# The router's index work put behind all four rankings, with expert units between its steps

## The chip, the cores and the metric

The kernel runs on one core of one Trainium2 chip. The metric is device microseconds of one execution; the median of three runs before the change is 3709.58 us (3703.13 to 3713.91).

The core's engines have their own in-order instruction queues and meet only through semaphores: TensorE (PE; its weight loads are PEld), VectorE (DVE), ScalarE (ACT), GpSimd (POOL) and SyncE (SP, which here only issues DMAs). ACT and POOL issue some DMAs too. An instruction that waits for something holds up everything behind it on its engine.

## The reference, cut to what matters

Two transformer blocks on 512 tokens of width 1024. The change lies in the first block's expert layer (`peer`), between a gated mixer before it and a second block of attention after it:

```
q = (hb @ w_q).reshape(T, 8, 2, 128)                    # 8 heads, two halves
s = einsum('thpc,hpnc->thpn', q, sub_keys)              # 128 scores per half
sub_s, sub_i = top_k(s, 16)
cand = (sub_s[:, :, 0, :, None] + sub_s[:, :, 1, None, :]).reshape(T, 8, 256)
top_s, top_i = top_k(cand, 16)                          # 16 of the 256 sums
k1 = take_along_axis(sub_i[:, :, 0], top_i // 16); k2 = take_along_axis(sub_i[:, :, 1], top_i % 16)
g = softmax(top_s)                                      # the gates
act = gelu(einsum('td,thkd->thk', hb, expert_u[k1 * 128 + k2])) * g
out = einsum('thk,thkd->td', act, expert_v[k1 * 128 + k2])
```

## The kernel before, in words

The expert layer (`experts`, L576) treats the 512 tokens in four tiles of 128. Tiles 0 to 2 (384 tokens) go the dense way: products of these tokens with all 16384 rows of `expert_u`, later weighted by a gate matrix and multiplied with `expert_v`. Tile 3 goes the sparse way: its 128 tokens' chosen rows are gathered from HBM by 256 indirect DMAs of 512 KB (`gathered`, L693), each followed by one VectorE instruction.

**Units.** The dense first half is 128 equal units (`up_products`, L732). One unit loads 512 KB of `expert_u` in two DMAs (`wr<-eu`, issued on SP), splits it into a rounded part `wh` (ACT cast, L120) and a rest `wl` (L122, on POOL; on VectorE while `dve_lo` holds the tag, as in the gate-matrix stage), runs 24 matmuls of 128x384 into a PSUM tile `u` (two of them), and evicts `u` through a Gelu on ACT into `hb` (L745), stored by an ACT DMA. Units have no data in common with the routing: they are filler, issued by `tick(n)` (L592), which adds n to a counter and traces one unit for each whole number. After the context stage the rest is traced in one loop (L619).

**Stages that call `tick`.** In `route` (L750): the scores (2 and 14 x R1 = 0.5), the ranking (R2 = 0.7 before each of 32 heads' rankings), 1.0, and the gate matrix (48 x R3 = 0.6, in the loop at L884). In `context` (L1446, the second block's context tokens), R4 = 0.53 before each of its 104 weight products (`mm`). Then 6 more in `unit` calls and the rest.

**The ranking, tile by tile (L814), in the order 3, 0, 1, 2.** Per tile VectorE builds 64 candidate sums per head (`cand`, L818), and ranks each head (`top16`, L667: MAX8, FIND_INDEX8, MATCH_REPLACE8, MAX8, FIND_INDEX8). Then comes the tile's index work (L826 to L847): small mask arithmetic, then twice a compare (L842) and a product (L844) of 128x2048 elements and a reduction (L846) into `kt`. Tile 3's two results make `xid`, the row numbers of the gathers. After the fourth tile the softmax runs over all tiles at once: a subtraction (L856, VectorE), an Exp on ACT (L857), a sum, a reciprocal and a product (VectorE), the copy of tile 3's gates on ACT (L862). Then nine transposes on PE (L867: two `kt` and one `e` per dense tile), each evicted on ACT into `k0T`, `k1T` or `k2T` (L868), and `kw`. The gate-matrix stage takes over their SBUF pool when it is closed.

**What sets the order.** Each engine's queue is laid out ahead of time by a planner: a list scheduler that takes the instructions in traced order as priority, simulates their durations with a cost model, and lets a later one go first where it is ready sooner in that simulation. `self.here(ins)` (L689) takes an instruction out of this: it is queued behind everything traced before it on its engine (later work may still be placed ahead of it). In the kernel before, the gathers and the VectorE instructions that follow them are so pinned; the Exp, the transposes and their evictions are not. `gathered` is a generator: its first gather is traced at the first `self.sparse` call (L900).

Of the kernel before, what the change touches and what calls it, by code (L numbers as in the profile page):

```python
# [8 lines left out]
F32 = mybir.dt.float32  # L9
# [4 lines left out]
U32 = mybir.dt.uint32  # L14
AF = mybir.ActivationFunctionType
# [1 line left out]
AX = mybir.AxisListType  # L17
PSUM = bass.MemoryType.PSUM

R1, R2, R3, R4, R5, R6 = 0.5, 0.7, 0.6, 0.53, 0.9, 0.12  # L20
PC = 2
MB, MD, MR = 4, 2, 1.15
TG, NT = 4, 8
# [11 lines left out]
GS = 32768.0  # L35
# [32 lines left out]
class Kern:  # L68
# [681 lines left out]
    def route(self, ws, pu, tick):  # L750
        nc, a, h = self.nc, self.a, self.h
        with ExitStack() as s1:
            ip = self.pool("ip", scope=s1)
            pr = self.pool("pr", 1, PSUM, s1)
# [7 lines left out]
            kT = [ip.tile([128, TD, 2], F16 if i < 2 else F32, name="k%dT" % i) for i in range(3)]  # L762
# [3 lines left out]
            with ExitStack() as s2:  # L766
                rp = self.pool("r1", scope=s2)
# [32 lines left out]
            def ax(t, pat, shape):  # L800
                return t.rearrange(pat, o=1).to_broadcast(shape)

            S4 = [128, 8, 16, 16]
            with ExitStack() as s2:
                rp = self.pool("r2", scope=s2)
# [5 lines left out]
                srcs = {}  # L811
                tva = rp.tile([128, 4, 8, 16], F32, name="tva")
                gates = self.sp_.tile([128, 128], F32, name="gates")
                for n in (3, 0, 1, 2):  # L814
                    cand = rp.tile([128, 8, 64], F32, name="cand", tag="cand", bufs=2)
                    for p0, i0, ni, nj in ROWS:
                        S = [128, 8, ni, nj]
                        nc.vector.tensor_tensor(cand[:, :, p0:p0 + ni * nj].rearrange("p h (i j) -> p h i j", j=nj),  # L818
                                                ax(vals[:, n, :, 0, i0:i0 + ni], "p h (i o) -> p h i o", S),
                                                ax(vals[:, n, :, 1, 0:nj], "p h (o j) -> p h o j", S), op=OP.add)  # L820
                    tv = tva[:, n]
                    ti = rp.tile([128, 8, 16], U32, name="ti", tag="ti", bufs=2)
                    for hd in range(8):
                        tick(R2)
                        self.top16(rp, cand[:, hd], 64, tv[:, hd, :], ti[:, hd, :], "mr2")
                    pos = rp.tile([128, 8, 16], F32, name="pos", tag="pos", bufs=2)  # L826
                    nc.vector.tensor_copy(pos, ti)
                    msk = rp.tile([128, 8, 16], F32, name="msk", tag="msk", bufs=2)
# [10 lines left out]
                    src = []  # L839
                    for w_, (at, table, cmp) in enumerate(((pos, st16, OP.is_ge), (col, io16, OP.is_equal))):  # L840
                        oh = rp.tile(S4, F32, name="oh", tag="oh", bufs=2)
                        nc.vector.tensor_tensor(oh, ax(at, "p h (r o) -> p h r o", S4),  # L842
                                                table.rearrange("p (o r) i -> p o r i", o=1).to_broadcast(S4), op=cmp)
                        nc.vector.tensor_tensor(oh, oh, ax(idf[:, n, :, w_, :], "p h (o i) -> p h o i", S4), op=OP.mult)  # L844
                        kt = rp.tile([128, 8, 16], F32, name="kt", tag="kt", bufs=8)
                        nc.vector.tensor_reduce(out=kt, in_=oh, axis=AX.X, op=OP.add)  # L846
                        src.append(kt)  # L847
                    if n == 3:
                        xid = self.sp_.tile([128, 128], I32, name="xid")
                        nc.vector.scalar_tensor_tensor(xid, src[1].rearrange("p h r -> p (h r)"), 128.0,  # L850
                                                       src[0].rearrange("p h r -> p (h r)"), op0=OP.mult, op1=OP.add)
                        self.sunits = self.gathered(xid, gates, htok)
                    srcs[n] = src
                e = rp.tile([128, 32, 16], F32, name="e")
                tv = tva.rearrange("p n h r -> p (n h) r")
                nc.vector.tensor_tensor(e, tv, tv[:, :, 0:1].to_broadcast([128, 32, 16]), op=OP.subtract)  # L856
                nc.scalar.activation(out=e, in_=e, func=AF.Exp)  # L857
                sm = rp.tile([128, 32], F32, name="sm")
                nc.vector.tensor_reduce(out=sm, in_=e, axis=AX.X, op=OP.add)
                nc.vector.reciprocal(sm, sm)  # L860
                nc.vector.tensor_tensor(e, e, ax(sm, "p (h o) -> p h o", [128, 32, 16]), op=OP.mult)
                nc.scalar.copy(gates, e[:, 24:32].rearrange("p h r -> p (h r)"))  # L862
                for n in range(3):
                    tps = pr.tile([128, 3, 128], F32, name="tps", tag="tps", bufs=2)
                    for i in range(3):
                        src = srcs[n][i] if i < 2 else e[:, 8 * n:8 * n + 8]
                        nc.tensor.transpose(tps[:, i, :], src.rearrange("p h r -> p (h r)"), self.ident)  # L867
                        nc.scalar.activation(out=kT[i][:, n * 128:(n + 1) * 128, :], in_=ax(tps[:, i, :], "p (t o) -> p t o", [128, 128, 2]),  # L868
                                             func=AF.Copy, scale=GS if i == 2 else 1.0)
                nc.scalar.copy(kw[0], kT[2])  # L870
                nc.vector.tensor_tensor(kw[1], kT[2], kw[0], op=OP.subtract)
            s12.close()
# [1 line left out]
            with ExitStack() as s2:  # L874
                rp = self.pool("r3", 2, scope=s2)
# [8 lines left out]
                for b in range(TD // 32):  # L884
                    stg = rp.tile([128, 128, 32], F32, name="stg", tag="stg")
                    for c in range(32 // NT):
                        t0 = b * 32 + c * NT
                        oh = []
                        for i in range(2):
                            o = rp.tile([128, NT, 128], F16, name="oh%d" % i, tag="oh%d" % i)  # L890
# [1047 lines left out]
```

## Time and profile before

| | us |
|---|---|
| runs shown | 3709.58 median, 3703.13 to 3713.91 |
| profiled execution, its own time | 3703.34 |
| its span, first to last instruction | 3701.6 |
| PE busy | 3415.2 (92% of the span) |
| VectorE busy | 2369.2 (64%) |
| ACT busy | 1564.2 (42%) |
| POOL busy | 1407.8 (38%) |
| mean granted TensorE clock | 0.966 |

The stages around the change, in us from the span's start: scores about 570 to 728, ranking and index work 728 to 857, gate matrix 857 to 1084, context from there to about 1690, the last units and the first products of the second half to 1745. From 1744 on PE runs the dense second half without a break until 2201; the second block follows.

Readings to keep apart: "busy" of PE is modelled, since matmuls are pipelined; a wait is put down to the instruction that released it last; a granted clock of 1.00 is 2.4 GHz, and 0.5 would be 1.2 GHz throughout.

### The profile page before, as it was taken

To read this page: it belongs to the slowest core of one execution; us is meant where nothing else is said; L and a number is where in the kernel's file an instruction comes from. 1 tells how busy PE (TensorE), PEld (TensorE's weight loads), DVE (VectorE), ACT (ScalarE), POOL (GpSimd) and SP (SyncE) were. 2 spreads that over 40 slices of the span, in tenths; PEclk is the share of its full clock that TensorE was granted. 3 is DMA by queue.
4 is the path that set the end of the run, shared out by engine and by line. 5 is a ranking of instruction groups with operands and counts; after the bars stand their busy time and mean duration, and the time that the engine had idled before them with its cause. 6 is when DMAs were issued, how large, how long until landed. Compare 5 with 4: busy or idle time off the path is not lost.

```text
span 3701.6 us, 54609 instructions
## 1 busy us (share of the span) xinstructions
PE 3415.2 (92%) x20219; PEld 3074.3 (83%) x20219; DVE 2369.2 (64%) x4572; ACT 1564.2 (42%) x2940; POOL 1407.8 (38%) x1178
## 2 busy tenths in 40 slices
PE   6999999978889998897999999899999979999998
PEld 5889788877788988897999998778878877787777
DVE  7876865698867765666777775444255664433554
ACT  3323223235654374642333333444346443442663
POOL 2210114352235667565222211554425335542442
PEclk9999999989999998998999999999999989999999
DMA  7667644337877856578999993322211321212122
GB/s 274 217 204 263 219 159 152 107 125 269 298 265 242 301 194 241 184 273 294 355 342 337 327 328 111 103 69 69 77 52 55 134 82 63 75 67 67 54 72 99
DMA packets 273243, 668.18 MB, mean 181 GB/s; under 512 B 25424, under 2 KB 88016, under 8 KB 270160
## 3 DMA queue, kind: packets, MB, share of 16 engines
q1 hardware_dynamic: 220256, 469.43, 36.9%
q0 software_dynamic: 36864, 134.23, 10.1%
q10 hardware_dynamic: 15856, 61.02, 4.3%
q8 instruction: 159, 2.61, 0.3%
q14 instruction: 108, 0.88, 0.1%
HBM read 601.47 MB, written 63.11 MB: 180 GB/s over the span
## 4 chain that ended last, share of the span: by engine, by line
PE 65%; DVE 13%; DMA 7%; issue 7%; ACT 5%; POOL 3%; SPq 0%; POOLq 0%; ACTq 0%; DVEq 0%
PE mm L95 16%; PE acc L95 12%; PE gm L95 10%; PE u L95 8%; PE cm L95 4%; PE uq L95 2%; PE sc L95 2%; PE pv L1168 2%; DMA wr<-eu 2%; PE tp L1138 2%; PE pv L95 2%; PE tp L95 1%; DVE wm L212 1%; DVE wl L122 1%; POOL wl L122 1%
## 5 line engine op out<-in xcount | busy, mean ns | idle before, releaser
L122 POOL TENSOR_TENSOR wl<-wr,wh 128x512 fp32r<-128x512 f32 (+3 forms) x358 | 499.0, 1411 | 452.3 <-ACT wh L120 437.6
L120 ACT CAST wh<-wr 128x512 fp32r<-128x512 f32 (+3 forms) x546 | 355.8, 665 | 576.2 <-PE mm L95 201.5
L95 PE MATMUL u<-hh,wh 128*128 128x384 f32 (+1 forms) x1040 | 361.5, 348 | 31.8 <-ACT hb L745 31.6
L95 PE MATMUL u<-hh,wl 128*128 128x384 f32 (+1 forms) x1040 | 360.2, 347 | 9.7 <-DVE wl L122 8.9
L95 PE MATMUL u<-hl,wh 128*128 128x384 f32 (+1 forms) x1040 | 358.8, 345 | 0.0
L95 PE MATMUL acc<-ah,vh 128*128 128x384 f32 x1024 | 343.9, 336 | 8.8 <-ACT hb L745 8.8
L95 PE MATMUL acc<-al,vh 128*128 128x384 f32 x1024 | 343.3, 335 | 0.9 <-DVE al L122 0.9
L95 PE MATMUL acc<-ah,vl 128*128 128x384 f32 x1024 | 343.2, 335 | 0.0
L714 POOL DMA_INDIRECT sg<-ev,xid x128 | 153.3, 1198 | 311.4 <-DVE sacc L729 258.0
L120 ACT CAST vh<-vr 128x1024 fp32r<-128x1024 f32 x128 | 134.6, 1052 | 316.8 <-issue 145.0
L714 POOL DMA_INDIRECT sg<-ur,xid x128 | 146.8, 1147 | 270.2 <-DVE sg L212 250.7
L95 PE MATMUL mm<-hh,wh 128*128 128x512 f32 (+2 forms) x608 | 239.3, 398 | 9.1 <-DVE sm L432 4.2
L122 DVE TENSOR_TENSOR wl<-wr,wh 128x1024 fp32r<-128x1024 f32 (+4 forms) x188 | 179.5, 972 | 101.2 <-ACT wh L120 100.1
L95 PE MATMUL mm<-hh,wl 128*128 128x512 f32 (+2 forms) x608 | 238.9, 393 | 5.6 <-DVE wl L122 4.5
L95 PE MATMUL mm<-hl,wh 128*128 128x512 f32 (+2 forms) x608 | 238.8, 393 | 5.4 <-POOL hl L122 5.4
L122 DVE TENSOR_TENSOR vl<-vr,vh 128x1024 fp32r<-128x1024 f32 x128 | 158.3, 1237 | 128.4 <-ACT vh L120 126.9
L95 PEld LDWEIGHTS u<-hh,wh 128*128 128x128 f32 x1040 | 203.6, 196 | 34.8 <-ACT hb L745 32.9
L95 PEld LDWEIGHTS u<-hh,wl 128*128 128x128 f32 x1040 | 203.3, 196 | 13.1 <-DVE wl L122 11.3
L729 DVE SCALAR_TENSOR_TENSOR sacc<-sg,wts,sacc 128x1024 f32<-128x1024 f32 x128 | 189.3, 1479 | 22.5 <-DMA sg<-ev,xid 19.0
L95 PEld LDWEIGHTS u<-hl,wh 128*128 128x128 f32 x1040 | 203.4, 196 | 0.4
L95 PEld LDWEIGHTS acc<-ah,vh 128*128 128x128 f32 x1024 | 193.1, 189 | 9.3 <-ACT hb L745 9.1
L95 PEld LDWEIGHTS acc<-al,vh 128*128 128x128 f32 x1024 | 193.1, 189 | 1.1 <-DVE al L122 1.1
(713 smaller groups left out, 9837.2 us busy)
## 6 DMA issues: line engine op xcount, KB each, us to landing
wr<-eu SPq DMA_DIRECT2D x256, 256.0 KB
vr<-ev SPq DMA_DIRECT2D x128, 512.0 KB
wm<-wmod SPq DMA_DIRECT2D x88, 512.0 KB
wr<-w SPq DMA_DIRECT2D x164, 256.0 KB
wr<-wA SPq DMA_DIRECT2D x80, 512.0 KB
wrc<-w SPq DMA_DIRECT2D x79, 512.0 KB
wrg<-w SPq DMA_DIRECT2D x104, 256.0 KB
hd<-hb ACTq DMA_DIRECT2D x64, 384.0 KB
```

The source lines that it names most:

```text
L95: ins = self.nc.tensor.matmul(ps, l, r, start=first and i == 0, stop=last and i == 2)
L120: nc.scalar.copy(hi, x)
L122: eng.tensor_tensor(lo, x, hi.bitcast(F32), op=OP.subtract)
L212: return self.nc.vector.scalar_tensor_tensor(chunk, chunk, 1.0, row, op0=OP.mult, op1=OP.mult, accum_out=dst)
L714: self.here(nc.gpsimd.indirect_dma_start(t, None, tabs[i], bass.IndirectOffsetOnAxis(idx[:, j:j + 1], 0)))
L729: self.here(nc.vector.scalar_tensor_tensor(acc, t, wts[:, j:j + 1], acc, op0=OP.mult, op1=OP.add))
L1138: nc.tensor.transpose(t[:, (b - i) * 128:(b - i + 1) * 128], p[:, b * 128:(b + 1) * 128], self.ident)
L1168: nc.tensor.matmul(o[:, lo:hi], v(b), pt[k][:, b, lo:hi], start=i == 0 and k == 0, stop=i == len(parts) - 1 and k == 1)
```

## The change

The loop over tiles is cut into three inner functions. `best(n)` is the candidate sums and the ranking of a tile; `keys_of(n)` its index work; `turn(n, i)` one transpose with its eviction, both now pinned with `self.here`. The order becomes: `best(3)`, `keys_of(3)` and `xid`; `best(0)`, `best(1)`, `best(2)`; the subtraction; `keys_of(0)`; the Exp (pinned); `keys_of(1)`; sum, reciprocal, product; two transposes of tile 0; `keys_of(2)`; the gates' copy, now on VectorE; the third transpose of tile 0 and the three of tile 1; `tick(R8)`; the three of tile 2. The tile `ti` becomes one slice per token tile (`tia`).

The units are dealt out anew: R2 from 0.7 to 0.45; a `tick(R7 / 2)` of 2 units twice in each `keys_of`; R8 = 2 units before the last transposes; R3 from 0.6 to 0.55; R4 from 0.53 to 0.47.

```diff
--- before.py
+++ after.py
@@ -17,7 +17,7 @@
 AX = mybir.AxisListType
 PSUM = bass.MemoryType.PSUM
 
-R1, R2, R3, R4, R5, R6 = 0.5, 0.7, 0.6, 0.53, 0.9, 0.12
+R1, R2, R3, R4, R5, R6, R7, R8 = 0.5, 0.45, 0.55, 0.47, 0.9, 0.12, 4, 2
 PC = 2
 MB, MD, MR = 4, 2, 1.15
 TG, NT = 4, 8
@@ -811,18 +811,22 @@
                 srcs = {}
                 tva = rp.tile([128, 4, 8, 16], F32, name="tva")
                 gates = self.sp_.tile([128, 128], F32, name="gates")
-                for n in (3, 0, 1, 2):
+                tia = rp.tile([128, 4, 8, 16], U32, name="tia")
+                order = (3, 0, 1, 2)
+
+                def best(n):
                     cand = rp.tile([128, 8, 64], F32, name="cand", tag="cand", bufs=2)
                     for p0, i0, ni, nj in ROWS:
                         S = [128, 8, ni, nj]
                         nc.vector.tensor_tensor(cand[:, :, p0:p0 + ni * nj].rearrange("p h (i j) -> p h i j", j=nj),
                                                 ax(vals[:, n, :, 0, i0:i0 + ni], "p h (i o) -> p h i o", S),
                                                 ax(vals[:, n, :, 1, 0:nj], "p h (o j) -> p h o j", S), op=OP.add)
-                    tv = tva[:, n]
-                    ti = rp.tile([128, 8, 16], U32, name="ti", tag="ti", bufs=2)
                     for hd in range(8):
                         tick(R2)
-                        self.top16(rp, cand[:, hd], 64, tv[:, hd, :], ti[:, hd, :], "mr2")
+                        self.top16(rp, cand[:, hd], 64, tva[:, n, hd, :], tia[:, n, hd, :], "mr2")
+
+                def keys_of(n):
+                    ti = tia[:, n]
                     pos = rp.tile([128, 8, 16], F32, name="pos", tag="pos", bufs=2)
                     nc.vector.tensor_copy(pos, ti)
                     msk = rp.tile([128, 8, 16], F32, name="msk", tag="msk", bufs=2)
@@ -842,31 +846,51 @@
                         nc.vector.tensor_tensor(oh, ax(at, "p h (r o) -> p h r o", S4),
                                                 table.rearrange("p (o r) i -> p o r i", o=1).to_broadcast(S4), op=cmp)
                         nc.vector.tensor_tensor(oh, oh, ax(idf[:, n, :, w_, :], "p h (o i) -> p h o i", S4), op=OP.mult)
+                        tick(R7 / 2)
                         kt = rp.tile([128, 8, 16], F32, name="kt", tag="kt", bufs=8)
                         nc.vector.tensor_reduce(out=kt, in_=oh, axis=AX.X, op=OP.add)
                         src.append(kt)
+                    return src
+
+                e = rp.tile([128, 32, 16], F32, name="e")
+                sm = rp.tile([128, 32], F32, name="sm")
+
+                def turn(n, i):
+                    if i == 0:
+                        tpss[n] = pr.tile([128, 3, 128], F32, name="tps", tag="tps", bufs=2)
+                    src = srcs[n][i] if i < 2 else e[:, 8 * n:8 * n + 8]
+                    self.here(nc.tensor.transpose(tpss[n][:, i, :], src.rearrange("p h r -> p (h r)"), self.ident))
+                    self.here(nc.scalar.activation(out=kT[i][:, n * 128:(n + 1) * 128, :],
+                                                   in_=ax(tpss[n][:, i, :], "p (t o) -> p t o", [128, 128, 2]),
+                                                   func=AF.Copy, scale=GS if i == 2 else 1.0))
+
+                tpss = {}
+                for n in order:
+                    best(n)
                     if n == 3:
+                        src = keys_of(3)
                         xid = self.sp_.tile([128, 128], I32, name="xid")
                         nc.vector.scalar_tensor_tensor(xid, src[1].rearrange("p h r -> p (h r)"), 128.0,
                                                        src[0].rearrange("p h r -> p (h r)"), op0=OP.mult, op1=OP.add)
                         self.sunits = self.gathered(xid, gates, htok)
-                    srcs[n] = src
-                e = rp.tile([128, 32, 16], F32, name="e")
                 tv = tva.rearrange("p n h r -> p (n h) r")
                 nc.vector.tensor_tensor(e, tv, tv[:, :, 0:1].to_broadcast([128, 32, 16]), op=OP.subtract)
-                nc.scalar.activation(out=e, in_=e, func=AF.Exp)
-                sm = rp.tile([128, 32], F32, name="sm")
+                srcs[0] = keys_of(0)
+                self.here(nc.scalar.activation(out=e, in_=e, func=AF.Exp))
+                srcs[1] = keys_of(1)
                 nc.vector.tensor_reduce(out=sm, in_=e, axis=AX.X, op=OP.add)
                 nc.vector.reciprocal(sm, sm)
                 nc.vector.tensor_tensor(e, e, ax(sm, "p (h o) -> p h o", [128, 32, 16]), op=OP.mult)
-                nc.scalar.copy(gates, e[:, 24:32].rearrange("p h r -> p (h r)"))
-                for n in range(3):
-                    tps = pr.tile([128, 3, 128], F32, name="tps", tag="tps", bufs=2)
-                    for i in range(3):
-                        src = srcs[n][i] if i < 2 else e[:, 8 * n:8 * n + 8]
-                        nc.tensor.transpose(tps[:, i, :], src.rearrange("p h r -> p (h r)"), self.ident)
-                        nc.scalar.activation(out=kT[i][:, n * 128:(n + 1) * 128, :], in_=ax(tps[:, i, :], "p (t o) -> p t o", [128, 128, 2]),
-                                             func=AF.Copy, scale=GS if i == 2 else 1.0)
+                for i in range(2):
+                    turn(0, i)
+                srcs[2] = keys_of(2)
+                nc.vector.tensor_copy(gates, e[:, 24:32].rearrange("p h r -> p (h r)"))
+                turn(0, 2)
+                for i in range(3):
+                    turn(1, i)
+                tick(R8)
+                for i in range(3):
+                    turn(2, i)
                 nc.scalar.copy(kw[0], kT[2])
                 nc.vector.tensor_tensor(kw[1], kT[2], kw[0], op=OP.subtract)
             s12.close()
```

## Rows read from the trace of the kernel before

**Rows 1.** The page's forty slices of the span, in tenths: PE.
```profile
PE   6999999978889998897999999899999979999998
```
**Rows 2.** Stretches by time: busy us (instructions) of PE, PEld, DVE, ACT, POOL; clock; DMA.
```profile
780.00:800.00 20.00, 20.00 (x118) 20.00 (x117) 20.00 (x47) 8.43 (x16) 16.27 (x11) 1.00 0.48 170
800.00:820.00 20.00, 6.05 (x35) 5.72 (x34) 20.00 (x64) 0.45 (x1) 0.88 (x1) 0.78 0.14 47
```
**Rows 3.** Waits of PE and ACT, 725 to 860: total us, times, longest.
```profile
PE u L95 <- ACT hb L745: 22.5, 1, 22.5
PE tps L867 <- ACT k0T L868: 5.4, 1, 5.4
...
ACT e L857 <- DVE e L856: 25.6, 1, 25.6
```
**Rows 4.** ACT in order of time: start, duration; idle time before, its releaser.
```profile
731.55 0.48 ACT L745 ACTIVATE hb<-u 128x384 f32<-128x384 f32 x1
...
798.16 0.49 ACT L745 ACTIVATE hb<-u 128x384 f32<-128x384 f32 x1
...
826.04 0.63 ACT L857 ACTIVATE e<-e 128x512 f32<-128x512 f32 x1 [25.59 <-DVE e L856]
...
840.15 0.30 ACT L862 COPY gates<-e 128x128 f32<-128x128 f32 x1 [4.84 <-DVE e L861]
```
**Rows 5.** VectorE in order of time: index work, softmax and the next stage's first.
```profile
764.35 1.37 DVE L850 SCALAR_TENSOR_TENSOR xid<-kt 128x128 int32<-128x128 f32 x1
...
772.71 0.22 DVE L827 CAST pos<-ti 128x128 f32<-128x128 uint32 x1
...
794.41 2.27 DVE L846 TENSOR_REDUCE kt<-oh 128x128 f32<-128x2048 f32 x1
...
803.37 0.22 DVE L827 CAST pos<-ti 128x128 f32<-128x128 uint32 x1
...
816.65 2.27 DVE L846 TENSOR_REDUCE kt<-oh 128x128 f32<-128x2048 f32 x1
...
825.34 0.67 DVE L856 TENSOR_TENSOR e<-tva 128x512 f32<-128x512 f32 x1
...
842.84 2.27 DVE L846 TENSOR_REDUCE kt<-oh 128x128 f32<-128x2048 f32 x1
...
856.55 0.69 DVE L891 TENSOR_TENSOR oh<-iota,k0T 128x1024 f16<-128x1024 f16 x1 [2.35 <-PE tps L867]
```
**Rows 6.** VectorE groups by form, 728 to 766: count, busy us, mean ns.
```profile
L844 DVE TENSOR_TENSOR oh<-oh,idf 128x2048 f32<-128x2048 f32 x2 | 6.6, 3282 | 0.0
...
L838 DVE CAST col<-mi 128x128 f32<-128x128 uint32 x1 | 1.2, 1174 | 0.0
```
**Rows 7.** The same groups, 802 to 826.
```profile
L844 DVE TENSOR_TENSOR oh<-oh,idf 128x2048 f32<-128x2048 f32 x2 | 4.6, 2276 | 0.0
...
L838 DVE CAST col<-mi 128x128 f32<-128x128 uint32 x1 | 0.2, 217 | 0.0
```
**Rows 8.** The tile wl, 728 to 860, its POOL instructions: ns min/median/max.
```profile
L122 POOL TENSOR_TENSOR wl<-wr,wh x38: 1287/1306/3434, 731.8 to 834.9; 128x512 fp32r<-128x512 f32 x38
```
**Rows 9.** The chain by line: 857 to 1084, 1108 to 1663, 1663 to 1745.
```profile
by line: DMA wr<-eu 24.0%; PE u L95 23.4%; DVE ow L895 8.9%; PE gps L904 8.3%; DVE oh L891 7.4%; ACT stg L906 7.0%; DVE wl L122 6.9%; issue 5.1%; DVE sg L212 4.4%; ACT wh L120 1.6%; DVE sacc L729 1.6%; ACT hb L745 1.4%; DVEq L122 0.1%; DVE 
...
by line: PE u L95 26.2%; PE cm L95 25.4%; issue 9.4%; DMA sg<-ev,xid 5.9%; DVE wlc L122 3.8%; DMA wrc<-w 2.9%; POOL wl L122 2.8%; POOL sz L1172 1.5%; ACT whc L120 1.3%; DMA sg<-ur,xid 1.3%; PE ct L1138 1.1%; DMA hd<-hb 1.1%; DVE sacc L729 1
...
by line: DMA vr<-ev 30.5%; POOL wl L122 16.0%; issue 10.0%; DMA wr<-eu 8.7%; PE u L95 7.3%; ACT wh L120 3.0%; POOL sg L714 2.7%; ACT vh L120 2.6%; PE cm L95 2.4%; SPq L87 2.3%; ACT hb L745 1.9%; DVE vl L122 1.5%; PE ct L171 1.5%; ACT sq L15
```
**Rows 10.** The tile hb: units evicted from 857 to 1084, 1108 to 1663, 1663 to 1745.
```profile
L745 ACT ACTIVATE hb<-u x30: 483/491/493, 857.7 to 1081.6; 128x384 f32<-128x384 f32 x30
...
L745 ACT ACTIVATE hb<-u x51: 478/487/496, 1125.6 to 1662.6; 128x384 f32<-128x384 f32 x51
...
L745 ACT ACTIVATE hb<-u x12: 468/485/492, 1662.6 to 1743.8; 128x384 f32<-128x384 f32 x12
```
**Rows 11.** POOL in order of time: the first gather.
```profile
836.40 1.14 POOL L714 DMA_INDIRECT sg<-ur,xid  x1 [0.16 <-DVE mi L836]
```

## The prediction

> **What bounds the kernel now.** I read the page's slices first: PE is at 9 tenths almost everywhere, so what counts is where PE stands still [rows 1]. The ninth and tenth slices, 740 to 833 us, are the lowest run of the first half's middle, and there VectorE is full. The stretches show why they differ: from 780 to 800 PE, PEld and VectorE are all at 20.00 of 20 us; from 800 to 820 PE has 6.05, and its clock has fallen from 1.00 to 0.78 [rows 2]. The waits name it: once, for 22.5 us, the units' matmuls waited for `hb`, the eviction that frees their PSUM tile; ACT, which does it, waited 25.6 us for the subtraction before the softmax [rows 3]. So the Exp stood in ACT's queue ahead of evictions that were due. In order of time: units evicted every 4.16 us ((798.16 - 731.55) / 16 intervals), then nothing until the Exp at 826.04 [rows 4]. VectorE was behind the plan: it subtracts at 825.34 [rows 5].
>
> After it VectorE finishes the last tile's index work at 845.1 (842.84 + 2.27), and the gate matrix starts only at 856.55, since its tiles take over the pool that the transposes still read [rows 5]. In between lie 5.4 us of PE for an eviction of a transpose [rows 3]. Last, the later stages: units' matmuls are 23.4%, 26.2% and 7.3% of the chains of the gate matrix, the context and the tail [rows 9].
>
> **Units, counted.** Traced before the gate matrix: 2 + 7 + 22.4 = 31 before; 2 + 7 + 14.4 + 16 + 2 = 41 after. In the gate matrix (with the `tick(1.0)`) 30 become 27, in the context 55 become 49, at its end 6 stay, and the rest falls from 6 to 5. Ten units move ahead, out of three later stages. The total of PE's work is unchanged: a gain is PE's standing still that goes, less what the later stages get back by losing filler.
>
> **The PE side of the new ranking.** The eviction at 731.55 is the 10th unit's, so 22 units precede the pinned Exp (31 in all), 4 more the first transposes, 4 the next, 2 the last. The 31st's eviction comes at 731.55 + 21 x 4.16 = 819, the 39th's at 852, the 41st's at 860.6. Does the pitch hold? It did, 16 times in a row, beside contended index work with POOL at 16.27 of 20 us and DMA at 170 GB/s [rows 2, 4]; ten more units bring ten more pairs of `wl` on POOL, ten `hb`, twenty casts and twenty SP loads at the same rate, and ACT has 8.43 of 20 us busy. So the units cost PE what they cost later, and SP's queue is only passed earlier by the same loads.
>
> **The VectorE side.** Work is the same but for the copy of the gates. Tile 0's index work took 24.0 us (772.71 to 796.68) with POOL splitting beside it, tile 1's 15.5 us (803.37 to 818.92) with POOL idle [rows 5]; the planner laid some of the next ranking between them, which I estimate at 2.3 and 1.2 us (its last candidate sum and a few small instructions). So 21.7 against 14.3. The products show it, 3282 against 2276 ns [rows 6, 7]. With units beside all four tiles I take 21 us for each. Tile 3's ends with `xid` at 765.7. Three rankings follow: before, the stretch from there to 825.34 held just them and the index work of tiles 0 and 1, so they take 59.6 - 21.7 - 14.3 = 23.6 us, and I add 1 for candidate sums that now meet POOL: 790, the subtraction to 791. Then tile 0 to 812, tile 1 to 833, tile 2 with softmax (about 4 us) to 858. The Exp needs 791 and has 819: its wait is gone. The first transposes (behind the 35th unit, about 836) need 812, tile 1's need 833 and stand at 853. Late next are two things: the product of the softmax, which the planner may put behind most of tile 2's index work (about 855) while the third transpose stands behind the 39th unit at 852, and tile 2's keys at 858 against 860.6.
>
> The Trainium skill, "SBUF — State Buffer", section "Who interferes with whom", says that a VectorE instruction with two SBUF inputs and a GpSimd one that reads SBUF exclude each other for a whole instruction. That speaks against this change, which puts POOL's splits beside index work that ran alone. The 3282 and 2276 ns agree; a rule of whole instructions, taken at its worst, is the end of my first rival.
>
> **The sum** (in the profiled execution's own time, 3703.34; the median shown is 6.2 us above it, and I carry the difference over).
> - Start of the gate matrix. PE ends the 41st unit about 860; 3 us for the third transpose's wait and 2.5 us for nine pinned transposes, each pair in one tile waiting for an ACT eviction: 866 instead of 856.55, +9.5. Bounds: +4 (no wait) and +17 (index work at 24 us a tile). A wait of a pinned transpose holds PE's and ACT's queues behind it, thus units and evictions, unless the planner put some ahead; their nearest row is the 5.4 us [rows 3].
> - Gathers. The first is queued on POOL behind the last split traced before it, now the 41st unit's: about 855 instead of 836.40 [rows 11], and the six at the start (3 MB) land as the gate matrix begins instead of ahead of it. Their consumer on VectorE has the copies behind it. Before, such loads met in the 5.4 us stall; I take nothing extra, bounds 0 and 6.
> - The gates' copy: ACT loses a wait of 4.84 us [rows 4] which by then held no matmul back; VectorE gains 0.2 us, or 1.2 if it meets POOL, by the nearest conversion of that size, 217 and 1174 ns [rows 6, 7]. The gates are first used after sixteen gathers. Nothing in the sum. (By the same section of the Trainium skill such a copy can take the shared port and block; a 1174 ns conversion beside POOL agrees.)
> - Gate matrix: 30 units over 227 us. Their matmuls, loads and splits are 23.4 + 24.0 + 6.9 = 54.3% of the chain [rows 9, 10], 123 us or 4.1 a unit, an upper end, since the loads also wait for the gathers. 2.5 units fewer (the 42nd is half begun), at 3 us: -7. Bounds 0 and -12.
> - Context: 26.2 + 2.8% of 555 us over 51 units is 3.15 us a unit [rows 9, 10]; 6 fewer: -19. Bounds: -6 (only a third comes back, filler having covered waits) and -25 (all 4.16).
> - Tail: one unit fewer: 16.0 + 8.7 + 7.3% of 82 us over 12 units is 2.2 us, and since no other products run beside the rest I take the pitch: -4; bounds -2 and -8.
>
> Together 9.5 - 7 - 19 - 4 = -20.5: 3682.8 for the profiled execution, 3689 as a median. As a check: 22.5 + 5.4 us of waits and a few us at the lower clock go, some 5 come, so PE is 25 to 28 us less idle there, and the later stages lose 4 to 8 of it.
>
> **Rivals.**
> 1. *VectorE is the bound of the new ranking.* If index work beside POOL takes 24 us a tile, as tile 0's whole stretch did, tile 2's keys come at 867 and PE and ACT stand behind the pinned transposes: the gate matrix starts 17 us late, 3697. At the worst each of about a dozen two-input or converting instructions of a tile waits for a whole split of 1.31 us [rows 8]: 14.3 + 12 x 1.31 = 30 us a tile, keys at 885, a start 31 us late and no gain, 3710. For: four tiles, not two and a half, meet POOL. Against: 24.0 us is the longest seen, with other work in it.
> 2. *All ten units come back in full.* 10 x 4.16 = 41.6, less 7.5: 3675. For: `u` and `cm`, PE's two kinds of product, make half of the context's chain [rows 9]. Against: the gate matrix's chain holds loads and copies too.
> 3. *The change doesn't do what it says*: another stall of some 20 us in the ranking takes the old one's place, the planner having set the pinned evictions too early for VectorE. Then +9.5 + 20 - 30 = about 3709. Against: the slack of 17 to 28 us worked out for all but the last two.
> 4. *Slower: the later stages do not give back.* If the context and the gate matrix are paced by loads, dependencies and VectorE, the units there are filler and cost nothing. The later start and gathers stay: 9.5 + 5 = +14, 3724. It decides from under 1.4 us returned per moved unit (14 / 10). For: loads and gathers have 24.0% of one chain and 5.9 + 2.9% of the other. Against: the `u` share of both [rows 9].
>
> **How the numbers follow.** Forecast 0.58, rivals 0.15, 0.12, 0.06 and 0.09. A measurement of this kernel can tell about 0.3%, 11 us: faster means below 3698.5. Forecast gives 0.54 of that (its bounds reach past the line a little), rival 2 all, rival 1 half: 0.74. Same: 0.04 + 0.07 + 0.06 = 0.17. Slower 0.09. The range holds forecast, rivals 1 and 2: 3672 to 3705.
>
> **What would show it.** In the trace after: no wait of PE for `hb` over 5 us between 728 and 866; the Exp directly after its table load; 41 evictions before the gate matrix's first compare, at 862 to 870; index work at 20 to 22 us in all four dense and gathered tiles; the context's stretch 15 to 22 us shorter. It would be wrong if the first compare came after 875, if the context kept its length with more idle PE, or if a pinned transpose took the Exp's place as the long wait.

## The result, and the profile after

The changed kernel takes 3669.81 us (median of 4 runs, 3662.54 to 3677.99) against 3707.3 us (median of 4, 3703.13 to 3713.91): a ratio of 0.991, with a 95% interval of 0.989 to 0.993. Timed again on another occasion beside the kernel before, it took 3668.8 against 3706.09 us, 0.9905 (0.9885 to 0.9926). So it is faster by 37 us, and its median lies 19 us below the forecast of 3689. It is also 2 us below the lower end of the range, 3672 to 3705; taken as a ratio from the 3709.58 that the forecast started from, it is 3676 (3669 to 3684), inside it. The result is at the range's edge either way. The profiled execution took 3676.05 us, 27.3 less than the one before (3703.34).

PE's slices of the changed kernel, in tenths, answer to [rows 1]. The ninth slice shows where to look: it had 7 tenths and has 9. (A slice is 92.5 us, so the prediction's 740 to 833 us is the ninth slice alone, not the ninth and tenth.)

```profile
PE   6999999998788989888999998999999979999998
```

The same two stretches as in [rows 2], 4 us later because the stages ahead took 4 us longer (their code is the same). Columns are the stretch, its length, busy us (instructions) of PE, PEld, DVE, ACT, POOL, granted clock, DMA share, GB/s:

```profile
784.00:804.00 20.00, 20.00 (x118) 20.00 (x117) 20.00 (x83) 7.60 (x15) 15.18 (x10) 1.00 0.48 156
804.00:824.00 20.00, 20.00 (x117) 20.00 (x117) 20.00 (x14) 7.39 (x15) 17.10 (x11) 1.00 0.59 195
```

The second had 6.05 us of PE at a clock of 0.78; now it is full at 1.00. What PE and ACT waited for, the changed kernel's answer to [rows 3] (PE from 728 to 880, where this is its only wait, ACT from 725 to 870; one line of each):

```profile
PE tps L862 <- DVE e L883: 5.1, 1, 5.1
...
ACT k2T L863 <- PE tps L862: 5.5, 2, 4.7
```

The 22.5 us for `hb` and ACT's 25.6 us for the subtraction are gone. What is late instead is the third transpose, which waits for the softmax's product. ACT in order of time [rows 4]:

```profile
735.91 0.48 ACT L745 ACTIVATE hb<-u 128x384 f32<-128x384 f32 x1
...
823.31 0.49 ACT L745 ACTIVATE hb<-u 128x384 f32<-128x384 f32 x1
823.82 1.28 ACT L879 ACT_TABLE_LOAD   x1
825.11 0.63 ACT L879 ACTIVATE e<-e 128x512 f32<-128x512 f32 x1
...
856.96 0.48 ACT L745 ACTIVATE hb<-u 128x384 f32<-128x384 f32 x1
...
873.32 0.49 ACT L745 ACTIVATE hb<-u 128x384 f32<-128x384 f32 x1
```

These are the evictions of the 10th, 31st, 39th and 41st unit. From the 10th to the 31st the pitch is (823.31 - 735.91) / 21 = 4.16 us, from there to the 39th 4.21; the last two take 16.4 us between the transposes. VectorE in order of time [rows 5]:

```profile
793.23 0.67 DVE L877 TENSOR_TENSOR e<-tva 128x512 f32<-128x512 f32 x1
...
857.59 2.29 DVE L851 TENSOR_REDUCE kt<-oh 128x128 f32<-128x2048 f32 x1
...
860.89 0.69 DVE L883 TENSOR_TENSOR e<-e,sm 128x512 f32<-128x512 f32 x1
861.62 0.23 DVE L887 COPY gates<-e 128x128 f32<-128x128 f32 x1
...
876.37 0.69 DVE L915 TENSOR_TENSOR oh<-iota,k0T 128x1024 f16<-128x1024 f16 x1
```

From the subtraction's start to the last reduction's end 66.7 us go to three tiles, 22.2 each. The product stands behind all of the last tile's index work. The first gather [rows 11] is behind the 41st unit's split:

```profile
858.85 1.14 POOL L714 DMA_INDIRECT sg<-ur,xid  x1 [0.17 <-issue]
```

**The ledger.** The chain of waits lists next to nothing of the changed kernel's gate matrix and context, so [rows 9] have no counterpart, and I count by stretches. They are cut where the work is the same in both kernels: first conversion of the ranking, first compare of the gate matrix, its last eviction, first addition of the context's merge, last product of the dense second half (its start, at 2284.8 before; the 2201 given above is not yet the end of that work). The kernel before:

```profile
730.50:856.50 126.00, 97.10 (x538) 95.28 (x537) 119.98 (x354) 39.72 (x78) 74.37 (x46) 0.89 0.45 157
856.50:1082.80 226.30, 191.13 (x1489) 176.12 (x1488) 199.92 (x313) 139.04 (x187) 58.94 (x40) 0.94 0.78 279
1082.80:1671.40 588.60, 530.39 (x3626) 514.59 (x3625) 388.73 (x571) 297.05 (x583) 365.64 (x298) 0.94 0.69 238
1671.40:2284.80 613.40, 592.21 (x3386) 588.84 (x3385) 452.16 (x611) 214.69 (x315) 153.07 (x138) 0.98 0.86 309
```

The changed kernel:

```profile
734.80:876.40 141.60, 136.49 (x777) 135.33 (x776) 133.06 (x356) 55.90 (x109) 110.45 (x65) 0.98 0.58 188
876.40:1088.40 212.00, 174.63 (x1409) 159.85 (x1408) 194.53 (x309) 133.28 (x179) 54.04 (x39) 0.95 0.80 284
1088.40:1650.80 562.40, 506.32 (x3491) 488.82 (x3491) 387.79 (x572) 288.51 (x566) 339.09 (x288) 0.96 0.72 244
1650.80:2254.40 603.60, 586.61 (x3362) 581.91 (x3361) 449.06 (x611) 212.80 (x312) 151.11 (x136) 0.99 0.87 312
```

PE's instruction counts add up to 9039 in both: the four stretches hold the same work. At 24 matmuls a unit, the ranking gained 239 / 24 = 10.0 units, and the others gave up 3.3, 5.6 and 1.0. Length less PE's busy time is PE's idle time: 28.9, 35.2, 58.2, 21.2 us before, 5.1, 37.4, 56.1, 17.0 after. The ranking lost 23.8 us of idling for its ten units, and the three stages that gave them up together idle 110.5 us instead of 114.6. That is the gain: -27.9 us of idle time, and -6.8 us of busy time for the same instructions, at a clock of 0.98 instead of 0.89 in the ranking and 0.96 instead of 0.94 in the context.

### The profile page after: what moved, and what is told of

The parts are those of the page before. It is cut to its first block, busy times and chain, and to the rows that moved or that the text cites. A ratio compares the mean times of both kernels' runs of the same rounds, so it can differ in the third digit from the quotient of the medians.

```text
span 3674.3 us, 54614 instructions
## 1 busy us (share of the span) xinstructions
PE 3414.1 (93%) x20219; PEld 3070.9 (84%) x20219; DVE 2371.5 (65%) x4567; ACT 1564.0 (43%) x2941; POOL 1410.4 (38%) x1184
## 4 chain that ended last, share of the span: by engine, by line
PE 39%; DMA 5%; issue 4%; DVE 4%; ACT 3%; POOL 1%; SPq 0%; POOLq 0%; ACTq 0%; DVEq 0%
PE acc L95 11%; PE gm L95 9%; PE mm L95 8%; PE pv L1192 2%; PE sc L95 2%; PE tp L1162 2%; PE pv L95 2%; PE tp L95 1%; DMA vr<-ev 1%; DMA wr<-w 1%; DMA wro<-w 1%; POOL wl L122 1%; PE sc L1417 0%; PE sc L1422 0%; ACT wh L120 0%
## 5 line engine op out<-in xcount | busy, mean ns | idle before, releaser
L122 POOL TENSOR_TENSOR wl<-wr,wh 128x512 fp32r<-128x512 f32 (+3 forms) x364 | 506.6, 1408 | 417.6 <-ACT wh L120 403.7
L95 PEld LDWEIGHTS acc<-ah,vl 128*128 128x128 f32 x1024 | 193.2, 189 | 1.3 <-DVE vl L122 1.3
```

What stands on the lines that cost most here:

```text
L95: ins = self.nc.tensor.matmul(ps, l, r, start=first and i == 0, stop=last and i == 2)
L122: eng.tensor_tensor(lo, x, hi.bitcast(F32), op=OP.subtract)
```

## The experiments

The rows of the table are profiled executions cut as above (ranking, gate matrix, context, tail with dense second half; us), beside the medians and ratios of the timed runs. "Units" are those traced before the gate matrix, in it, in the context and in the rest after the six at its end; "idle" is PE's, in the ranking and in the other three. The ratio is to the kernel before as timed beside each.

| kernel | median | ratio (95%) | units | stretches | idle |
|---|---|---|---|---|---|
| before | 3707.3 | 1 | 31, 30, 55, 6 | 126, 226, 589, 613 | 29 + 115 |
| the change | 3669.81 | 0.991 (0.989-0.993) | 41, 27, 49, 5 | 142, 212, 562, 604 | 5 + 110 |
| the change again | 3668.80 | 0.9905 (0.9885-0.9926) | the same | 142, 213, 565, 606 | 5 + 114 |
| order and pins only | 3704.60 | 0.9998 (0.9984-1.0011) | 31, 30, 55, 6 | 123, 225, 600, 613 | 22 + 127 |
| units only | 3688.23 | 0.9950 (0.9933-0.9966) | 41, 27, 49, 5 | 162, 212, 563, 605 | 24 + 105 |
| no pins | 3680.09 | 0.9926 (0.9908-0.9944) | 41, 27, 49, 5 | 156, 218, 563, 604 | 18 + 107 |
| Exp pinned | 3699.81 | 0.9983 (0.997-0.9996) | 31, 30, 55, 6 | 124, 220, 594, 613 | 23 + 118 |
| gates on ACT | 3685.64 | 0.9947 (0.9928-0.9966) | 41, 27, 49, 5 | 159, 215, 562, 604 | 22 + 111 |
| softmax first | 3669.52 | 0.9908 (0.9889-0.9928) | 41, 27, 49, 5 | 140, 216, 560, 605 | 5 + 110 |
| units in gate matrix | 3678.27 | 0.9927 (0.9906-0.9947) | 41, 30, 49, 2 | 142, 225, 570, 593 | 5 + 116 |
| units in context | 3662.33 | 0.9888 (0.9868-0.9909) | 41, 27, 55, 0 | 142, 213, 584, 585 | 5 + 118 |
| fewer in gate matrix | 3679.28 | 0.9931 (0.9912-0.9951) | 41, 25, 49, 7 | 140, 203, 578, 615 | 5 + 118 |
| more in index work | 3668.20 | 0.9909 (0.9887-0.9931) | 45, 27, 49, 1 | 155, 216, 559, 591 | 4 + 114 |
| none before last turn | 3680.11 | 0.9927 (0.9907-0.9946) | 39, 27, 49, 7 | 140, 215, 565, 615 | 11 + 110 |

A letter in an expectation names a theory: A is mine, B or C a rival.

Differences from the change are between medians. For the four kernels that come out 9 to 11 us slower, the intervals of the ratio overlap that of the change. Run against run, six of each against the ten of the change, the change is the faster in 51 to 56 of 60 pairs.

**The new order and its pins, without the units.** The change with the old deal of units:

```diff
-R1, R2, R3, R4, R5, R6, R7, R8 = 0.5, 0.45, 0.55, 0.47, 0.9, 0.12, 4, 2
+R1, R2, R3, R4, R5, R6, R7, R8 = 0.5, 0.7, 0.6, 0.53, 0.9, 0.12, 0, 0
```

> The new order with its pinned Exp and transposes, but the units dealt out as before (R2 0.7, none in the index work, R3 0.6, R4 0.53): 31 units are traced before the gate matrix. Theory A (the gain is ten units moved under VectorE's work, and the order only makes room for them): the 31st eviction comes at about 819 us, PE then stands until the index work is over, and the gate matrix starts a few us earlier than before since less index work meets POOL's splits: 0 to 10 us faster than the kernel before. Theory B (the gain is the 22.5 us stall behind the Exp, and the new dealing-out is only a rebalancing): 20 us or more faster.

No difference (0.9998). The wait for `hb` is gone, and another of its size is there. First line: a wait of PE (us, times, longest); then a wait and an instruction of ACT, and the split on VectorE:

```profile
PE u L95 <- DVE wl L122: 24.4, 3, 19.8
...
ACT wh L120 <- DMA wr<-eu: 34.6, 10, 25.5
...
842.56 0.62 ACT L120 CAST wh<-wr 128x512 fp32r<-128x512 f32 x1 [25.55 <-DMA wr<-eu]
...
839.25 0.68 DVE L122 TENSOR_TENSOR wl<-wr,wh 128x512 fp32r<-128x512 f32 x1
```

The 31 units of the ranking run out early, and the next one belongs to the gate-matrix stage, whose splits are VectorE's: its `wl` starts at 839.25, when all of the index work but the last reduction is done. The order without units to fill it moves the stall from ACT's queue to VectorE's.

**The units alone.** The kernel before with the new numbers, all 41 units at the heads' rankings:

```diff
-R1, R2, R3, R4, R5, R6 = 0.5, 0.7, 0.6, 0.53, 0.9, 0.12
+R1, R2, R3, R4, R5, R6 = 0.5, 1.0125, 0.55, 0.47, 0.9, 0.12
```

> The old order, Exp and transposes not pinned, with the new numbers of units: R2 1.0125 (32.4 in the rankings), R3 0.55, R4 0.47. Theory A: the Exp still stands behind the 26th eviction, so the stall of some 22 us stays; 41 units must end before the transposes, so the gate matrix starts near 890 instead of 857, and the later stages give back about 50 us (what the run of the change showed): 10 to 20 us faster than before. Theory C (the numbers of units do it all, the order is indifferent): as fast as the change, 30 us or more.

18 us faster. Two waits and the Exp:

```profile
PE u L95 <- ACT hb L745: 20.4, 1, 20.4
...
ACT e L857 <- DVE e L856: 23.5, 1, 23.5
...
827.27 0.63 ACT L857 ACTIVATE e<-e 128x512 f32<-128x512 f32 x1 [23.55 <-DVE e L856]
```

The old stall is still there, nearly whole, but the later stages are as short as in the change (212 and 563). So part of the gain is not the stall. Ten units lengthened the ranking by 36 us, 3.6 each, since some fell into idle PE (28.9 to 23.7 us) and its clock rose from 0.89 to 0.93, while the three later stages gave back 48.

**The change without its pins**: `self.here` taken off the Exp, the transposes and their evictions.

```diff
-self.here(nc.tensor.transpose(tpss[n][:, i, :], src.rearrange("p h r -> p (h r)"), self.ident))
-self.here(nc.scalar.activation(out=kT[i][:, n * 128:(n + 1) * 128, :],
+nc.tensor.transpose(tpss[n][:, i, :], src.rearrange("p h r -> p (h r)"), self.ident)
+nc.scalar.activation(out=kT[i][:, n * 128:(n + 1) * 128, :],
...
-self.here(nc.scalar.activation(out=e, in_=e, func=AF.Exp))
+nc.scalar.activation(out=e, in_=e, func=AF.Exp)
```

> The change without the pins on the Exp, the transposes and their evictions. Theory A: the planner, which takes VectorE's index work as faster than it is beside POOL, puts the Exp far ahead, ACT waits some 20 us for the subtraction and PE with it, the gate matrix starts 15 to 20 us later than in the change: 15 to 20 us slower than the change. Rival: with the subtraction ahead of three tiles' index work the Exp is early enough anyway, and the pins are worth nothing: within 5 us of the change.

11 us slower than the change, where A said 15 to 20: right in kind, too large in size. The Exp stands behind the 19th eviction instead of the 31st:

```profile
PE u L95 <- ACT hb L745: 14.4, 1, 14.4
...
ACT e L879 <- DVE e L877: 17.0, 1, 17.0
```

**The pin alone**: the kernel before with `self.here` on its Exp.

```diff
-nc.scalar.activation(out=e, in_=e, func=AF.Exp)
+self.here(nc.scalar.activation(out=e, in_=e, func=AF.Exp))
```

> The kernel before with one pin, on the Exp, so that it stands behind the 31st eviction. Theory A: the 22.5 us wait of PE for the eviction shrinks to under 8 us, but PE only stands later, since no units are left before the transposes, and VectorE, which sets the start of the gate matrix, now meets more of POOL's splits: within 6 us of the kernel before. Theory B: the stall was the loss, so 15 us or more faster.

6.7 us faster, barely clear of noise (up to 0.9996) and just past A's 6. As in the first experiment the stall becomes one for a split on VectorE:

```profile
PE u L95 <- DVE wl L122: 25.7, 2, 21.7
```

The first experiment holds order and pins together, so the parts are these: order with pins 2 us (no difference that can be told), units 18, order with units but without pins 26, all three 37. The two halves alone add up to 20; the other 17 come only where units and order are together. The one pin in the old order brings 7. Units and pins in the old order were not tried.

**The gates' copy back on ACT**, at its place in the new order:

```diff
-nc.vector.tensor_copy(gates, e[:, 24:32].rearrange("p h r -> p (h r)"))
+nc.scalar.copy(gates, e[:, 24:32].rearrange("p h r -> p (h r)"))
```

> The change with the copy of tile 3's gates back on ACT. As predicted (the copy is worth nothing): within 4 us of the change. Theory A (ACT's queue is the place where a late VectorE holds up PE): the copy is queued behind the 32nd eviction, at about 829 us, and waits for the product of the softmax at about 861; ACT stands some 30 us, PE, two PSUM tiles further, some 20: 15 to 22 us slower than the change.

17 us slower than the change. Two waits and the copy:

```profile
PE u L95 <- ACT hb L745: 19.7, 1, 19.7
...
ACT gates L887 <- DVE e L883: 23.9, 1, 23.9
...
850.68 0.30 ACT L887 COPY gates<-e 128x128 f32<-128x128 f32 x1 [23.89 <-DVE e L883]
```

A copy of 0.30 us takes the Exp's place as the stall: it waits 23.9 us for the late product, with the evictions of the units behind it. The copy on VectorE took 0.23 us and held nobody.

**The softmax first**: its sum pinned, and the first instruction of tile 2's index work pinned behind it.

```diff
-nc.vector.tensor_reduce(out=sm, in_=e, axis=AX.X, op=OP.add)
+self.here(nc.vector.tensor_reduce(out=sm, in_=e, axis=AX.X, op=OP.add))
...
-nc.vector.tensor_copy(pos, ti)
+cp = nc.vector.tensor_copy(pos, ti)
+if pin:
+    self.here(cp)
...
-srcs[2] = keys_of(2)
+srcs[2] = keys_of(2, True)
```

> The change with the sum, the reciprocal and the product of the softmax pinned on VectorE ahead of tile 2's index work. The change's PE waited 5.1 us for the product, which the planner had laid behind all of that index work. Theory A: the wait goes, the 41st unit and the gate matrix come 4 to 6 us earlier: 3 to 6 us faster than the change. Rival: VectorE's last reduction, at about 862 in either order, sets the start: within 2 us of the change.

The same as the change. The wait for the product goes, another of PE, for the eviction of a transpose, comes, and the ranking is only 2 us shorter, as the rival said:

```profile
PE tps L864 <- ACT k0T L865: 4.1, 1, 4.1
```

**Where the units go.** First R3 back to 0.6 (three units from the rest into the gate matrix):

```diff
-R1, R2, R3, R4, R5, R6, R7, R8 = 0.5, 0.45, 0.55, 0.47, 0.9, 0.12, 4, 2
+R1, R2, R3, R4, R5, R6, R7, R8 = 0.5, 0.45, 0.6, 0.47, 0.9, 0.12, 4, 2
```

> The change with R3 back at 0.6: three units more in the gate matrix, three fewer in the rest at the end (2 instead of 5). In the change the gate matrix was 14 us shorter for three units fewer, the tail with the dense half 10 us shorter for one. Theory A (those are the stages' prices, 4.8 and up to 9.8 us a unit): the gate matrix 14 us longer, the tail 15 us or more shorter: 1 to 12 us faster than the change. Rival (the tail's 10 us were mostly a change in how the second half starts, and a unit costs PE's 4.2 us in either place): the same as the change, within 3 us.

9 us slower, by neither theory: the gate matrix grew by 13 us and the context by 7, the tail shrank by 10. Next R4 back to 0.53 (the context takes the rest's units):

```diff
-R1, R2, R3, R4, R5, R6, R7, R8 = 0.5, 0.45, 0.55, 0.47, 0.9, 0.12, 4, 2
+R1, R2, R3, R4, R5, R6, R7, R8 = 0.5, 0.45, 0.55, 0.53, 0.9, 0.12, 4, 2
```

> The change with R4 back at 0.53: six units more in the context, six fewer after it (none in the rest). Theory A (a unit costs PE's pitch, about 4.2 us, in the context, as the three kernels with the new numbers show, 26 us for six; and about 4 in the tail): the context 25 us longer, the tail with the dense half 20 to 25 us shorter: within 6 us of the change. Rival (a tail unit costs more, 8 to 10 us, as the first one taken away seemed to): 15 us or more faster than the change.

The lowest median, but its interval overlaps that of the change, and it is the faster in only 37 of 50 pairs of runs; context +21, tail -19. Then R3 = 0.5 on top of the softmax first:

```diff
-R1, R2, R3, R4, R5, R6, R7, R8 = 0.5, 0.45, 0.55, 0.47, 0.9, 0.12, 4, 2
+R1, R2, R3, R4, R5, R6, R7, R8 = 0.5, 0.45, 0.5, 0.47, 0.9, 0.12, 4, 2
```

> The change with the softmax pinned ahead of tile 2's index work, and R3 down to 0.5: two or three units fewer in the gate matrix, as many more in the rest. Three more in the gate matrix cost 9 us net in an earlier run. Theory A (a unit's price there, 4 us, hardly differs from the tail's, and the 9 us were a shift of the context's plan): within 4 us of the change. Rival (units in the gate matrix cost more than elsewhere, since their splits fall on VectorE): 6 to 10 us faster than the change.

10 us slower: the gate matrix lost 13 us against the softmax first, the context gained 18, with 12 us more idle PE in it, and the tail 10. R7 = 5, four units more beside the index work:

```diff
-R1, R2, R3, R4, R5, R6, R7, R8 = 0.5, 0.45, 0.55, 0.47, 0.9, 0.12, 4, 2
+R1, R2, R3, R4, R5, R6, R7, R8 = 0.5, 0.45, 0.55, 0.47, 0.9, 0.12, 5, 2
```

> The change with R7 = 5: 45 instead of 41 units ahead of the gate matrix, 1 instead of 5 in the rest. Theory A (the ranking stage is now paced by PE, and VectorE ends about 12 us before the gate matrix can start): the gate matrix starts 16 to 18 us later, the tail is 15 to 18 us shorter: within 4 us of the change. Rival (VectorE still covers more units): 10 us or more faster.

No difference: the ranking took 13 us more, the tail 12 less, since the ranking had hardly any idle PE left to fill (5.1 us). Last, R8 = 0 on top of the softmax first:

```diff
-R1, R2, R3, R4, R5, R6, R7, R8 = 0.5, 0.45, 0.55, 0.47, 0.9, 0.12, 4, 2
+R1, R2, R3, R4, R5, R6, R7, R8 = 0.5, 0.45, 0.55, 0.47, 0.9, 0.12, 4, 0
```

> The change with the softmax pinned ahead of tile 2's index work and R8 = 0: 39 units ahead of the gate matrix, two more at the end. Theory A: VectorE's last reduction, at about 860 us, and PE's 39th unit now end together; the gate matrix starts 7 to 9 us earlier, and the two units cost 8 us in the tail: within 3 us of the change. Rival (PE stands during the last transposes without them): 4 us or more slower.

11 us slower, and the ranking no shorter. Two waits of PE, 725 to 900:

```profile
PE tps L864 <- ACT k0T L865: 7.1, 1, 7.1
PE u L95 <- DVE wl L122: 5.9, 2, 3.5
```

The two units before the last transposes cost nothing there: without them PE idled in their place, 10.6 us instead of 4.5, and they were paid for in the tail, 615 instead of 605. And the change once more, for the spread:

> The change itself, timed on the same chip as the three others: 3670 us as in its first runs, within 6.

Its stretches came within 2.3 us of those of the first profile.

## Why the prediction was right in sign and short in size

**The stall.** Right: the Exp comes directly after its table load, behind the 31st eviction, at 825.11; PE has no wait for `hb` in the ranking. Of order, units and pins, leaving out the units leaves 24.4 us of waits of PE, leaving out the pins 14.4, leaving out the order and the pins 20.4.

**The start of the gate matrix.** Forecast +9.5 (4 to 17), measured +15.6 for the stretch: 876.37, or 872.0 with the 4.36 us taken off that the stages ahead took longer (the 10th eviction at 735.91 instead of 731.55). The window of 862 to 870 was missed, and by the clock of the trace my own mark for "wrong", 875, was passed; by the stage's length it was not. PE did pace it, with one wait for VectorE's product in it. The last eviction of a unit is 12.7 us behind the 860.6 of the forecast, 8.4 without the shift. The 3 us for the product were 5.1. The 2.5 us for the transposes were 6.0: 2.9 between the 39th and the 41st eviction beyond two pitches and the wait (16.36 - 8.32 - 5.11), and 3.1 from the 41st to the first compare. Some 2 of the 2.9 are the clock, which the sum left out. After PE had stood for 5.1 us the granted clock was 0.50, the lower of its two levels, and 13 matmuls of a unit started 0.32 us apart instead of 0.17:

```profile
861.60:866.40 4.80, 4.76 (x17) 4.55 (x18) 2.67 (x5) 1.64 (x5) 3.89 (x4) 0.50 0.93 299
```

**Index work.** 22.2 us a tile against 21, a little over the 20 to 22 of the forecast, and no bound: rival 1 did not happen. Groups of VectorE by form, 786 to 863, the answer to [rows 6, 7], with one from 802 to 826 of the kernel before (L835, the same instruction as L839); then POOL's splits, 728 to 864 (count: ns min/median/max), to [rows 8]:

```profile
L848 DVE TENSOR_TENSOR oh<-oh,idf 128x2048 f32<-128x2048 f32 x6 | 20.2, 3369 | 0.0
L851 DVE TENSOR_REDUCE kt<-oh 128x128 f32<-128x2048 f32 x6 | 13.7, 2275 | 0.0
...
L839 DVE TENSOR_SCALAR mi<-msk 128x128 uint32<-128x128 f32 x3 | 4.0, 1318 | 0.0
...
L835 DVE TENSOR_SCALAR mi<-msk 128x128 uint32<-128x128 f32 x1 | 0.2, 216 | 0.0
...
L122 POOL TENSOR_TENSOR wl<-wr,wh x60: 1279/1303/3428, 729.0 to 855.4; 128x512 fp32r<-128x512 f32 x60
```

The six products are slowed, 3369 ns against 2276 alone, and POOL's median split is not. The Trainium skill, "SBUF — State Buffer", section "Who interferes with whom", has a VectorE instruction with two SBUF inputs and a GpSimd one that reads SBUF exclude each other; the trace agrees for the products, which take 1.1 us longer each beside the splits. That is 2.2 of the 7.9 us by which a tile's index work exceeds the 14.3 us that I estimated for the one that ran alone. The rest lies in its small instructions: those of 128x128 elements take 4.8 us a tile more than from 802 to 826 before, since half of them, 12 of 24, are longer by some 1.1 us each (1318 ns instead of 216 in the line shown); the compares take 0.4 more.

**Gathers.** The first came at 858.85, less the shift 854.5, against 855; the gate matrix's idle PE went from 35.2 to 37.4 us. Putting them at nothing in the sum was right within some 2 us.

**The gates' copy.** Wrong: I put it at nothing, because in the old order the wait of 4.84 us held no matmul back. In the new order the same instruction on ACT costs 17 us. I priced it by the row of before, where the softmax came late in the ranking and its units had run out, and did not ask what stands behind it after the move. The sum did not suffer, since the change does move the copy.

**What the later stages give back.** This is the mis-sized term. Forecast -7, -19 and -4, together -30; measured -14.3, -26.2 and -9.8, together -50.3, each beyond its bound. (The bounds were 12, 25 and 8.) I had sized a unit of the gate matrix and the context by its share of the chain, 3 and 3.15 us, and the tail's by the pitch, 4. The counts were a smaller part of it: the gate matrix gave up 3.3 units, not 2.5. But the idle time of PE in these stages hardly moved with the units: 114.6 before, 110.5 and 113.9 in two profiles of the change, 105 to 118 in every kernel but the one with order and pins only (127). So a unit that leaves takes its whole PE time with it: the gate matrix and the context gave up 8.96 units by the counts and 40.5 us, 4.5 each, a little over the pitch of 4.16 us. That pitch was read at a clock of 1.00; at the 0.94 of these stages it would be 4.16 / 0.94 = 4.4, by my estimate. The units' own instructions (tile `u`; the context has a few others by that name) show where it went. Gate matrix and context, before:

```profile
856.50:1082.80 226.30, 146.54 (x720) 128.37 (x720) 0.00 (x0) 14.66 (x30) 0.00 (x0) 0.94 0.78 279
1082.80:1671.40 588.60, 259.21 (x1330) 236.85 (x1329) 9.84 (x24) 36.37 (x80) 21.95 (x16) 0.94 0.69 238
```

And after:

```profile
876.40:1088.40 212.00, 131.84 (x641) 113.81 (x640) 0.00 (x0) 13.24 (x27) 0.00 (x0) 0.95 0.80 284
1088.40:1650.80 562.40, 232.30 (x1195) 209.66 (x1195) 9.84 (x24) 33.42 (x74) 20.84 (x16) 0.96 0.72 244
```

They take 41.6 us less of PE in the two stages, and the stages are 40.5 us shorter: the rest of PE's work and its idle time came out even. The sum of the two stages was 774.4 and 777.7 in the two profiles and 775.0 to 780.6 in the four experiments with the same units, 814.9 before. Rival 2, all ten units back in full at 3675, was closest in mechanism; even it took the pitch of the full clock (its "less 7.5" has no working; with the sum's 9.5 it is 3677).

The 4.5 us is not a constant. In the later experiments six units more in the context made it 21.4 us longer, 3.5 each by the counts. The gate matrix grew by 12.9 us for 2.9 units and shrank by 13.0 for 1.75, 4.4 and 7.4 each. In the tail three to six units fewer gave 3.1 to 3.5 each, and two more cost about 5 each.

**The tail** gave 9.8 us for one unit, 4.2 of it idle time (21.2 to 17.0) and 5.6 busy time. Waits of PE, 1671 to 1745 before:

```profile
PE u L95 <- ACT hb L745: 9.1, 3, 8.2
PE acc L95 <- ACT hb L745: 8.8, 1, 8.8
```

And after, 1650 to 1720:

```profile
PE acc L95 <- ACT hb L745: 3.2, 1, 3.2
...
PE u L95 <- ACT hb L745: 0.8, 1, 0.8
```

The last units' evictions held PE 17.9 us before and 4.0 after. Most of that came back as waits for the second half's own casts and splits, 0.9 us before and 10.6 after, over the whole stretch. With 5 units in the rest the stretch took 604 to 606 us in all six such profiles, with 6 or 7 units 613 to 615, with 2 or fewer 585 to 593. Why the step lies between 6 and 5 was not tried.

**The sum.** -34.7 in the four stretches against -20.5 (-29.0 in the second profile of the change); the unchanged stages ahead and the second block took 4.3 and 3.1 us more in that execution, which leaves the -27.3 of the profiled runs, and the medians say -37. What stays open: why three units more or two fewer in the gate matrix change the context's length by 7 and 18 us, with the same units in it. An order that the planner lays out anew for every deal of units would do that; no run shows it.

## What to carry to other kernels

Filler is worth its full engine time wherever that engine's idle time does not depend on it: count the idle time of each stage before and after, and price a moved unit by its pitch at the clock of the stage that it leaves, not by its share of the chain of waits. Here that would have been 4.4 us where 4.5 came back; single deals of units gave 3.1 to 7.4, so leave a wide range. Put filler where the engine idles, until it no longer does: ten units filled it here, and four more changed nothing. And whenever producers move, ask again who stands behind each consumer in its engine's queue: a 0.3 us copy that cost nothing in one order cost 17 us in the other.

## What the runs showed of the hardware that I had not expected

Beside POOL's splits VectorE's products of two 128x2048 operands took 3369 ns instead of 2276, but the reductions over as many elements kept 2275 (2270 in [rows 5], with POOL idle); only some of POOL's splits paid (up to 3428 ns, median 1303). The price was the same 1.1 us for a product of 2.3 us and for a small instruction of 0.2, close to the 1.3 us of one split; an instruction that waits until the split under way has ended would do that, which no run here separates from other causes. And a kernel does not repeat to the microsecond: in the two profiles of the change the stages ahead of the ranking took 734.8 and 731.7 us and the second block 1420 and 1410, most of the spread of all fourteen profiles (730.4 to 735.3, 1410 to 1420). So a term of a few us can be read from a stage's own length only, never from two spans.
